# Two more load slots at the start of the experts, and expert steps merged two by two, in a two-layer hybrid decoder

## The chip, the cores and the metric

The kernel runs on one core of a Trainium2 chip. The metric is the time on the device in microseconds. The time before is the median of three runs. The profile is of one execution. PE is TensorE, DVE is VectorE, ACT is ScalarE, POOL is GpSimd, and SP (SyncE) issues nearly all loads.

## The reference

Two layers on 256 tokens of width 1024, in fp32. Each layer has a token mixer (two attention branches behind one input projection, sigmoid gates, one output projection) and a channel mixer: a dense SwiGLU in layer 0, and 8 experts with 2 for each token in layer 1. Behind each sub-layer stands a LayerNorm over the residual.

```
def moe_swiglu(x, w_router, w_gate_up, w_down):
    logits = (x @ w_router).astype(jnp.float32)
    top_v, top_i = lax.top_k(logits, TOP_K)
    gates = jax.nn.softmax(top_v, axis=-1)
    combine = jnp.sum(jax.nn.one_hot(top_i, N_EXPERTS, dtype=jnp.float32) * gates[..., None], axis=-2)
    y = jnp.zeros_like(x)
    for e in range(N_EXPERTS):
        y = y + combine[..., e:e + 1].astype(x.dtype) * swiglu(x, w_gate_up[e], w_down[e])
    return y

for l in range(DEPTH):
    mix = token_mixer(h, w_in[l], ...)
    h = layer_norm(DEEPNORM_ALPHA * h + mix, ln_mix_g[l], ln_mix_b[l])
    f = swiglu(h, ...) if l % 2 == 0 else moe_swiglu(h, ...)
    h = layer_norm(DEEPNORM_ALPHA * h + f, ln_ffn_g[l], ln_ffn_b[l])
```

An expert's gate and up weights are 1024 x 7168, its down weights 3584 x 1024; all eight experts are read, about 350 MB.

## The kernel before

**Products.** Weights arrive as fp32 tiles (`raw`). In the dense layers and for the large experts each tile is split into a high part (`whi`, made on ACT, L433) and the remainder (`wlo`, made on DVE from `raw` and `whi`, L434). An fp32 product is then three fast ones: high by high and high by low of the activations (`xh`, `xl`), and low weights by `xh`. Products with few tokens use `raw` directly with fp32 activations (`xs`), where an instruction shows as two records. Nearly all products have L304, the helper that issues them, so they are told apart by tile names.

**The experts.** The experts of a run are sorted by the number of their tokens into eight places with 192, 128, 128, 64, 64, 32, 32 and 32 token slots (`SLOTS`). The last place always holds expert 7 (`FIXED`), whose weights can be loaded before the routing is known. Places 0, 1 and 2 form the big chain, with split weights; places 7, 6, 5, 4, 3 the small chain, with `raw`. A step of a chain is one load of up to 1 MiB and what is computed with it. Place 0 has 64 of its 192 slots apart (`far`): they are multiplied with `raw` directly, `mm<-raw,xs` with 64 columns, so a big tile's slot is free once its splits and its far product are done.

**Loads.** SP issues the loads in program order; each waits, on SP, until its slot is free. There are nine tiles in a pool of their own (`AHEAD`) and a ring of eight slots of 1 MiB (`RING`). The fixed expert's gate and up weights come as 32 tiles (8 for each of four column groups, `WIDE`): the first half is 16 tiles of 1 MiB, then come tiles of 768 KB. 17 tiles are fetched ahead (L382): seven of the first half and the first of the second in the ring, nine in the other pool. All later loads are from L389. When the first half is done, `self.front` is closed: the space of the nine tiles goes to the pool `parts`, which holds the high parts, while the low parts lie beside the ring in `wp`.

**Order.** The small chain's first eight steps (two tiles each) run first. Then `merge` takes steps of both chains, in proportion, by the counts of `MERGE`: (42 big, 47 small), (50, 14), (42, 46). A scheduler orders the instructions on each engine by priorities and dependences; `in_turn` chains only the products of one step, or of steps that `together` has joined, so steps can pass each other on PE.

**The final LayerNorm's rows.** `spread_rows` (from step 160) loads the weight and bias rows to one partition and multiplies them with a row of ones to get them on 128 partitions (L304, `tp<-ln_gb,one_row`), all four in one go, and ACT copies them out (L1613).

**Fillers.** `keep_busy` issues products whose results nobody reads (`o<-onesb`), in places where PE would stand idle. `out_norm` is the output projection with the LayerNorm behind it: for each of two token tiles statistics, a scale by small steps on DVE (`ln_scale`), then `ln_apply` (L545, L546), transposes and splits into `hT` for the next projection.

Of the kernel before, what the change touches and what calls it, by code (L numbers as in the profile page):

```python
# [9 lines left out]
F32R = mybir.dt.float32r  # L10
# [9 lines left out]
KT = D // 128  # L20
# [13 lines left out]
FIXED = 7  # L34
SLOTS = [192, 128, 128, 64, 64, 32, 32, 32]
UPS = (0, 6, 2, 8, 4, 10, 12)
RING, AHEAD = 8, 9
BRANCH, LEAD = 2, 6
MERGE = ((42, 47), (50, 14), (42, 46))
WIDE = ((0, 4), (7, 4), (4, 3), (11, 3))  # L40
# [39 lines left out]
class Packed:  # L80
# [138 lines left out]
    def last(self, keys, ws, st):  # L219


        nc, b, half = self.nc, self.b, self.half
        back = b.got[self.name][1].bitcast(F32)
        y = self.last_y(self.dn)
        bks = [[b.mm_bank() for _ in range(2)] for _ in range(2)]
        for t in range(2):
            b.in_turn([(bks[h][t], back[half[h], t * 128:(t + 1) * 128], y[half[h]], True, False) for h in range(2)])

        def products(x, ks, w, first, last):
            out = []  # L230
            for i, (r, _, j) in enumerate(ks):
                out += self.times([(x[half[i % 2]], 512 * i, 512)], self.hid[r, j], w, first and i < 2, last and i >= len(ks) - 2)
            b.in_turn(out, [w.load])

        def give(h, t, y):
            cs = slice(h * 512, h * 512 + 512)
            b.mm(bks[h][t], back[:, t * 128:(t + 1) * 128], y, False, True)
            nc.vector.scalar_tensor_tensor(self.acc[t][:, cs], bks[h][t], self.gates[t][:, self.place:self.place + 1], self.acc[t][:, cs],  # L238
                                           op0=OP.mult, op1=OP.add)
            b.ln_stats(self.acc[t], st[t], h)  # L240
        with b.tc.manual_schedule(engines={mybir.EngineType.PE}):
            xs = [b.aux_bank() for _ in range(2)]
            products(xs[0], keys, ws[0], True, True)
            y0 = self.last_y(xs[0])
            products(xs[1], keys[:2], ws[1], True, False)
            give(0, 0, y0)
            products(xs[1], keys[2:], ws[2], False, True)
            y1 = self.last_y(xs[1])
            give(0, 1, y0)
            for t in range(2):  # L250
                give(1, t, y1)
# [18 lines left out]
class Body:  # L270
# [114 lines left out]
    def slot(self, src, split=False):  # L385

        m, n = src.shape[1:]
        raw = self.raw()
        self.loaded = self.nc.sync.dma_start(raw[:, :m * n].rearrange("p (a b) -> p a b", b=n), src)  # L389
        w = Slot(raw, m * n, self.loaded)  # L390
        if split:
            for a in range(0, w.size, 1024):
                n = min(1024, w.size - a)
                both = [pool.tile([128, 1024], F32R, name="w" + p, tag="w" + p, bufs=4) for p, pool in (("hi", self.pp), ("lo", self.wp))]
                for p, x in zip("hl", both):
                    w.part[p].append(x)
                self.parted = self.split(both[0][:, :n], both[1][:, :n], raw[:, a:a + n])
        return w
# [335 lines left out]
    def mixer(self, l, xT):  # L734
# [7 lines left out]
        for i, k0 in enumerate((0, 2, 4, 6)):  # L742
            wpc = self.piece(w[:, k0:k0 + 2, C_FV:C_FV + 520], self.hold if i else self.first)
            for t in range(2):
                for hf in range(2):
                    if i == 0:
                        vps[t, hf] = self.aux_bank() if hf else self.mm_bank()
                    self.tok(vps[t, hf][:, :260], xT, k0, wpc, t, hf * 260, hf * 260 + 260, i == 0, i == 3)
        if l == 0:
            with tc.issue_after(self.made.ins):  # L750
                self.setup_bias()
# [202 lines left out]
    def out_norm(self, h, xT, w, nk, g, b, routed=False):  # L954
# [24 lines left out]
                    self.nc.vector.scalar_tensor_tensor(r[t][:, cs], h[t][:, cs], ALPHA, ps[t, hf], op0=OP.mult, op1=OP.add)  # L979
                    self.ln_stats(r[t], st[t], hf)  # L980

        def norm(t):
            if t == 0:
                out.extend(self.stream("hT"))
            return self.ln_apply(r[t], self.ln_scale(st[t]), gb,
                                 lambda hf: self.put_T([out[0][p, hf] for p in "hl"], r[t][:, hf * 512:(hf + 1) * 512], t))
        order = [(i, hf) for hf in range(2) for i in range(len(cuts))]
        for p in order[:-4]:
# [27 lines left out]
        with self.tc.manual_schedule(engines={mybir.EngineType.PE}):  # L1016
            for i in range(3):
                load(*p[i])
                go(*p[i], 0, 0)
                go(*p[i], 0, 1)  # L1020
            load(*p[3])
            for n, (i, part, t) in enumerate(((0, 0, 1), (0, 1, 1), (1, 0, 1), (3, 0, 0), (3, 1, 0), (1, 1, 1), (2, 0, 1), (2, 1, 1), (3, 0, 1), (3, 1, 1))):
                go(*p[i], t, part)
                for f, *x in behind.get(n, ()):
                    if routed and n == 9:
                        self.keep_busy(3, spare)
                    f(*x)
            self.keep_busy(11 if routed else 3, spare)
        if routed:
            scales = []  # L1030
            lg = self.rt.tile([128, 2, 8], F32, name="lg")
# [11 lines left out]
                self.ln_apply(r[1], scales[1], gb, lambda hf: None)  # L1043
            return r, (hot, routing)
        with self.tc.high_priority():
            self.hold = norm(0)
        self.first, self.late = None, self.hold
        norm(1)
        return r, out[1]


# [216 lines left out]

    def tile_mm(self, outs, x, w, flats, first, last):

        for n, out in enumerate(outs):
            for i, act in enumerate(x):
                for j, part in ((0, "h"), (1, "h")):
                    self.mm(out, act[j], w.at(part, flats[i] + n * 512, 512), first and i + j == 0, False)
        for n, out in enumerate(outs):
            for i, act in enumerate(x):
                self.mm(out, act[0], w.at("l", flats[i] + n * 512, 512), False, last and i == len(x) - 1)

    def together(self, products=(), loads=()):

        products, loads = list(products), list(loads)
        for p, l in self.beside:
            products += p
            loads += l
        self.beside = []
        if products:
            self.in_turn(products, loads)

    def settle(self):

# [4 lines left out]
    def in_turn(self, products, after=()):  # L1295

        made = []
        for x in products:
            self.mm(*x)
            made.append(self.made.ins)  # L1300
        for x in after:
            self.behind(made[0], x.ins, mybir.DependencyClass.Sync)
        for x, y in zip(made, made[1:]):
            self.behind(y, x, mybir.DependencyClass.NoSync)

    def behind(self, ins, other, kind):
        self.tc.add_manual_dep(ins, other.name, mybir.DependencyInfo(kind, mybir.DependencyReason.DATA), reason="order")
# [166 lines left out]
    def moe(self, ctx, h, routing, g, b):  # L1474
# [15 lines left out]

        self.banks(ctx, "experts_ps", mm=4, tp=2, aux=2)
        pool = self.pk = self.wk
        self.ahead(self.wp, "raw", RING, self.tiles[:2 * KT - AHEAD] + self.tiles[2 * KT:RING + AHEAD])
        eidi = next(routing)
        self.put_off, self.nrows = [], 5
        acc = []
        gates = []
        eid = {}
# [29 lines left out]
        def merge(x, y, parts, lead):  # L1528

            i = j = 0  # L1530
            ends = [(sum(p[0] for p in parts[:n + 1]), sum(p[1] for p in parts[:n + 1])) for n in range(len(parts))]
            at = (0, 0)
            for n, (ex, ey) in enumerate(ends):
                ly = ey - (lead if n == len(ends) - 1 else 0)
                while i < ex or j < ey:
                    if i < ex and (i - at[0]) * (ly - at[1]) <= (j - at[1]) * (ex - at[0]):
                        i += 1
                        yield next(x)
                    else:
                        j += 1  # L1540
                        yield next(y)
                at = ex, ey
        big = chain((0, 1, 2), (self.mm_bank, self.tp_bank))
        small = chain((7, 6, 5, 4, 3), (self.aux_bank, self.tp_bank))
# [2 lines left out]
        def both_chains():  # L1547
# [3 lines left out]
                yield next(small)  # L1551
            self.front.close()
            self.pp = self.side(self.later, "parts")
            yield from merge(big, small, MERGE, 8)
        for n, z in enumerate(both_chains()):
            if n == 6:
# [14 lines left out]
            if n == 72:  # L1571
                order.close()
            if n == 160:
                gb = self.spread_rows(g, b)
            if n == 14:
                with tc.issue_after(self.parted[0].ins):
                    for t in range(2):
# [21 lines left out]
    def spread_rows(self, g, b):  # L1599

        nc = self.nc
        one = self.wk.tile([1, 128], F32, name="one_row", bufs=1)
        nc.gpsimd.memset(one, 1.0)
        gb = [[self.pp.tile([128, 512], F32, name="ln_gb", tag="far", bufs=4) for _ in range(2)] for _ in range(2)]
        for row, xs in zip((g, b), gb):
            for hf, x in enumerate(xs):
                nc.sync.dma_start(x[0:1], row[None, hf * 512:(hf + 1) * 512])

        def f():
            for x in gb[0] + gb[1]:  # L1610
                bk = self.tp_bank()
                self.mm(bk, one, x[0:1], True, True)
                nc.scalar.activation(x, bk, AF.Copy)  # L1613
        self.later_on(f)
        return gb

    def overflow(self, h, gates, overi, most, weights, eid, acc):

# [85 lines left out]
    def dense(self):  # L1704
# [28 lines left out]
        h = xs  # L1733
        self.late = last
        for l in range(DEPTH):
            mT, wo = self.mixer(l, hT)
            if l == DEPTH - 1:
                self.tiles = [(p, k) for p in range(len(WIDE)) for k in range(KT)]
                self.ready = {}
                self.ahead(self.side(self.front, "ahead"), "ahead", AHEAD, self.tiles[2 * KT - AHEAD:2 * KT])  # L1740
            h, hT = self.out_norm(h, mT, wo, KT, a["ln_mix_g"][l], a["ln_mix_b"][l], l == DEPTH - 1)
            if l == 0:
                fT = self.ffn(hT)
# [28 lines left out]
```

## Time and profile before

| | |
|---|---|
| median of three runs | 1463.91 us (1463.39 to 1464.29) |
| profiled execution | 1463.79 us, its span 1462.1 us |
| mean granted PE clock | 0.989 |
| PE / DVE / ACT busy | 1399.9 / 812.4 / 655.4 us |
| bytes moved | 453.42 MB, mean 310 GB/s |
| fixed expert's first product | 617.52 us |
| last expert load lands | 1441.1 us |

A busy PE includes modelled ends of pipelined products, so the share alone doesn't say whether PE or the loads set the pace. The page cuts the span into 40 slices, which show the granted clock and the bytes; windows of a few microseconds show the same for a chosen stretch. A row of the timeline joins like instructions: start, time from the first start to the last end, engine, line, tiles, count.

### The profile page before, as it was taken

The numbers are of one execution on the slowest core, as the hardware profiler recorded it, in microseconds if no ns is written. First come the engines' busy times: TensorE is split into PE (matmuls) and PEld (weight loads), VectorE is DVE, ScalarE is ACT, GpSimd is POOL, SyncE is SP. The second block draws the span as 40 slices with busy tenths as digits, with TensorE's granted clock in tenths as the row PEclk, the third lists the DMA queues.
The fourth block names the chain that finished last, engine by engine and source line by source line (L and its number), as shares of the span: only waits on it lengthen the run. The fifth ranks groups of instructions, "written<-read, shape, count | busy, mean of one in ns | idle before, by whom it ended". The sixth has DMA issues, their size and how long they took to land. (4 is left out here: it accounts for less than half of the span.)

```text
span 1462.1 us, 20101 instructions
## 1 busy us (share of the span) xinstructions
PE 1399.9 (96%) x7581; PEld 929.2 (64%) x7581; DVE 812.4 (56%) x1233; ACT 655.4 (45%) x954; POOL 16.9 (1%) x44
## 2 busy tenths in 40 slices
PE   8999999999999999999999999999999999999985
PEld 6878978888788789755444453467675455445531
DVE  7757786665577676624253443377667245344423
ACT  4656546664266663133433332356555233323310
POOL 4000000000000000000000000000000000000000
PEclk9999999999999999999999999999999899999998
DMA  9633546555384347699999999999999899999994
GB/s 297 220 120 135 181 146 205 198 167 207 106 265 151 115 145 300 253 385 407 405 418 415 415 419 422 420 419 418 418 420 420 331 421 409 421 420 420 419 366 189
DMA packets 135767, 453.42 MB, mean 310 GB/s; under 512 B 8079, under 2 KB 63399, under 8 KB 108013
## 3 DMA queue, kind: packets, MB, share of 16 engines
q1 hardware_dynamic: 134872, 450.99, 79.5%
q0 software_dynamic: 784, 1.05, 0.4%
q8 instruction: 62, 1.02, 0.3%
q14 instruction: 45, 0.36, 0.1%
q10 hardware_dynamic: 4, 0.01, 0.0%
HBM read 450.96 MB, written 1.05 MB: 309 GB/s over the span
## 5 line engine op out<-in xcount | busy, mean ns | idle before, releaser
L434 DVE TENSOR_TENSOR wlo<-raw,whi 128x1024 fp32r<-128x1024 f32 (+2 forms) x456 | 516.6, 1161 | 414.7 <-ACT whi L433 402.5
L433 ACT ACTIVATE whi<-raw 128x1024 fp32r<-128x1024 f32 (+2 forms) x456 | 442.1, 1005 | 380.9 <-DMA raw<-in_w_expert_gate_up 140.4
L304 PE MATMUL mm<-hT,whi 128*128 128x512 f32 x672 | 234.8, 398 | 0.0
L304 PE MATMUL aux<-raw,xs 128*32 128x512 f32 (+3 forms) x1280 | 188.1, 552 | 4.3 <-DMA raw<-in_w_expert_gate_up 3.5
L304 PE MATMUL mm<-hT,wlo 128*128 128x256 f32 x672 | 175.8, 281 | 0.0
L304 PE MATMUL mm<-whi,xh 128*128 128x512 f32 x336 | 140.7, 419 | 4.7 <-ACT whi L433 3.4
L304 PEld LDWEIGHTS mm<-hT,whi 128*128 128x128 f32 x672 | 121.5, 188 | 23.8 <-issue 0.7
L304 PE MATMUL mm<-whi,xl 128*128 128x512 f32 x336 | 133.2, 396 | 0.0
L304 PEld LDWEIGHTS mm<-hT,wlo 128*128 128x128 f32 x672 | 126.8, 189 | 9.1 <-issue 2.0
L304 PEld LDWEIGHTS aux<-raw,xs 128*32 128x32 f32 (+1 forms) x1280 | 57.4, 121 | 108.6 <-issue 99.4
L304 PE MATMUL aux<-raw,eh 128*32 128x512 f32 (+1 forms) x560 | 93.0, 604 | 11.3 <-DMA raw<-in_w_expert_down 7.7
L304 PE MATMUL mm<-wlo,xh 128*128 128x512 f32 x336 | 98.7, 402 | 0.8 <-DVE wlo L434 0.7
L304 PEld LDWEIGHTS mm<-whi,xh 128*128 128x128 f32 x336 | 63.4, 189 | 56.6 <-issue 23.2
L304 PE MATMUL mm<-whi,eh 128*128 128x512 f32 x336 | 89.1, 405 | 5.6 <-ACT whi L433 5.6
L304 PEld LDWEIGHTS mm<-whi,eh 128*128 128x128 f32 x336 | 59.7, 188 | 36.7 <-ACT whi L433 18.6
L304 PEld LDWEIGHTS mm<-wlo,xh 128*128 128x128 f32 x336 | 62.2, 189 | 23.1 <-DVE wlo L434 4.6
L304 PEld LDWEIGHTS mm<-whi,xl 128*128 128x128 f32 x336 | 63.5, 189 | 11.7
L304 PEld LDWEIGHTS aux<-raw,eh 128*32 128x32 f32 (+1 forms) x560 | 26.2, 121 | 60.7 <-issue 58.2
L429 ACT ACTIVATE sums<-mm 128x512 f32<-128x512 f32 x84 | 50.2, 600 | 31.9 <-PE mm L304 30.5
L304 PE MATMUL aux<-hT,whi 128*128 128x512 f32 x160 | 56.2, 396 | 0.0
L304 PE MATMUL mm<-raw,xs 128*64 128x512 f32 x224 | 54.2, 605 | 0.0
L304 PE MATMUL mm<-whi,hT 128*128 128x260 f32 (+2 forms) x192 | 50.9, 335 | 1.2 <-DVE hT L434 0.9
(345 smaller groups left out, 1607.8 us busy)
## 6 DMA issues: line engine op xcount, KB each, us to landing
raw<-in_w_expert_gate_up SPq DMA_DIRECT2D x140, 1024.0 KB, 11.9
raw<-in_w_expert_down SPq DMA_DIRECT2D x111, 1024.0 KB, 12.7
raw<-in_w_expert_gate_up SPq DMA_DIRECT2D x112, 768.0 KB, 11.5
raw<-in_w_in SPq DMA_DIRECT2D x36, 1024.0 KB, 5.1
raw<-in_w_ffn_gate_up SPq DMA_DIRECT2D x22, 1024.0 KB, 5.1
raw<-in_w_ffn_down SPq DMA_DIRECT2D x10, 1024.0 KB, 4.9
raw<-in_w_out SPq DMA_DIRECT2D x8, 1024.0 KB, 5.0
raw<-in_w_in SPq DMA_DIRECT2D x8, 520.0 KB, 6.7
```

Of the source, the lines that this page charges most:

```text
L304: self.made = self.nc.tensor.matmul(out, lhsT, rhs, start=start, stop=stop)
L429: self.nc.scalar.activation(x, bank, AF.Copy, scale=scale)
L433: return (self.nc.scalar.activation(hi, src, AF.Copy), self.nc.vector.tensor_sub(lo, src, hi.bitcast(F32)))
L434: self.nc.vector.tensor_sub(lo, src, hi.bitcast(F32)))
```

## The change

Five things change together.

- `EXTRA = 2`: a second pool of two slots holds the last two tiles of the first half, until the first half is done. The nine tiles ahead are those before them, and the ring starts with five tiles of the first half and three of the second. From then on that space is the pool `low`, which holds the low split parts.
- `merge` takes two steps of a chain at a time. `in_line` chains all weight products on PE in program order, where before only the products of a step were chained.
- `spread_rows` splits each row into high and low parts and multiplies these with ones; the four spreads are given out one by one, every fourth step from step 160 on, each one flush behind its split.
- In layer 0's first column group eight fillers stand ahead of the transposes of a token tile. `out_norm` without routing has nine fillers, not three.
- `out_norm` computes the second token tile's scale ahead of the first tile's `ln_apply`.

```
-RING, AHEAD = 8, 9
+RING, AHEAD, EXTRA = 8, 9, 2
...
-                both = [pool.tile([128, 1024], F32R, name="w" + p, tag="w" + p, bufs=4) for p, pool in (("hi", self.pp), ("lo", self.wp))]
+                both = [pool.tile([128, 1024], F32R, name="w" + p, tag="w" + p, bufs=4) for p, pool in (("hi", self.pp), ("lo", self.lo))]
...
+                if l == 0 and i == 2 and t == 0:
+                    self.keep_busy(8, self.o_bank(), self.made)
...
-            self.keep_busy(11 if routed else 3, spare)
+            self.keep_busy(11 if routed else 9, spare)
...
-            self.hold = norm(0)
+            self.hold = norm(0, self.ln_scale(st[0]))
+            scale = self.ln_scale(st[1])
         self.first, self.late = None, self.hold
-        norm(1)
+        norm(1, scale)
...
+    def in_line(self, products, after=()):
+        made = self.in_turn(products, after)
+        if self.line:
+            self.behind(made[0], self.line, mybir.DependencyClass.NoSync)
+        self.line = made[-1]
...
-        self.ahead(self.wp, "raw", RING, self.tiles[:2 * KT - AHEAD] + self.tiles[2 * KT:RING + AHEAD])
+        early = 2 * KT - AHEAD - EXTRA
+        self.ahead(self.wp, "raw", RING, self.tiles[:early] + self.tiles[2 * KT:2 * KT + RING - early])
+        extra = self.front.enter_context(tc.tile_pool(name="extra", bufs=1, reuse_waits="tile"))
+        self.ahead(extra, "extra", EXTRA, self.tiles[2 * KT - EXTRA:2 * KT])
...
-                        i += 1
-                        yield next(x)
+                        for _ in range(min(2, ex - i)):
+                            i += 1
+                            yield next(x)
                     else:
-                        j += 1
-                        yield next(y)
+                        for _ in range(min(2, ey - j)):
+                            j += 1
+                            yield next(y)
...
             self.front.close()
             self.pp = self.side(self.later, "parts")
+            self.lo = ctx.enter_context(tc.tile_pool(name="low", bufs=1, reuse_waits="tile"))
...
-                gb = self.spread_rows(g, b)
+                gb, spreads = self.spread_rows(g, b)
+            if n > 160 and n % 4 == 0 and spreads:
+                self.later_on(spreads.pop(0))
...
-        def f():
-            for x in gb[0] + gb[1]:
-                bk = self.tp_bank()
-                self.mm(bk, one, x[0:1], True, True)
-                nc.scalar.activation(x, bk, AF.Copy)
-        self.later_on(f)
-        return gb
+                def f(x=x):
+                    parts = [self.row_tile("parts", F32R)[0:1] for _ in range(2)]
+                    self.split(*parts, x[0:1])
+
+                    def spread():
+                        bk = self.tp_bank()
+                        self.in_turn([(bk, oner, p, i == 0, i == 1) for i, p in enumerate(parts)])
+                        nc.scalar.activation(x, bk, AF.Copy)
+                    self.later_on(spread)
+                spreads.append(f)
+        return gb, spreads
```

On SP, the loads ahead and the first ones behind them, before. 128x2048 is a tile of the first half, 128x1536 one of the second, 128x2x1024 a tile of the big chain; an ISA row sets up the address of the routed expert.

```order
L382 DMA raw<-in_w_expert_gate_up 128x2048 x16
L382 DMA raw<-in_w_expert_gate_up 128x1536
L1512 TENSOR_LOAD eidi
L1512 ISA x2
L1560 TENSOR_LOAD omaxi
L1560 ISA x2
L389 ISA
L389 DMA raw<-in_w_expert_gate_up 128x2x1024
L389 DMA raw<-in_w_expert_gate_up 128x1536 x3
L389 ISA
L389 DMA raw<-in_w_expert_gate_up 128x2x1024
L389 DMA raw<-in_w_expert_gate_up 128x1536 x2
```

The same place after the change.

```order
L382 DMA raw<-in_w_expert_gate_up 128x2048 x14
L382 DMA raw<-in_w_expert_gate_up 128x1536 x3
L382 DMA raw<-in_w_expert_gate_up 128x2048 x2
L1528 TENSOR_LOAD eidi
L1528 ISA x2
L1579 TENSOR_LOAD omaxi
L1579 ISA x2
L389 ISA
L389 DMA raw<-in_w_expert_gate_up 128x2x1024
L389 ISA
L389 DMA raw<-in_w_expert_gate_up 128x2x1024
L389 DMA raw<-in_w_expert_gate_up 128x1536 x5
```

Two tiles of the second half have moved ahead of the routing, and the second big tile stands directly behind the first. The last two of the five 128x1536 loads take the slots of the two big tiles.

On PE, behind the first half, before. The `aux` products of 32x512 belong to the first half, those of 32x384 to the second; `mm_6275` is the big chain's bank.

```order
L304 MATMUL aux_6187<-raw_5708,xs_6075 32x512 x4
L304 MATMUL aux_6299<-raw_6073,xs_6075 32x384 x4
L304 MATMUL aux_6299<-raw_6297,xs_6075 32x384 x4
L304 MATMUL aux_6299<-raw_6312,xs_6075 32x384 x4
L304 MATMUL aux_6299<-raw_6314,xs_6075 32x384 x4
L148 MATMUL tp_6290<-ident_123,rows_6250 128x128 x4
L304 MATMUL mm_6275<-whi_6267,xh_6139 128x512
L304 MATMUL mm_6275<-whi_6267,xl_6140 128x512
L304 MATMUL mm_6276<-whi_6267,xh_6139 128x512
L304 MATMUL mm_6276<-whi_6267,xl_6140 128x512
L304 MATMUL mm_6289<-raw_6265,xs_6141 64x512 x4
```

After the change, from the end of the second big step on (the first half's last product is followed by 24 products of the two big steps, `mm_6307` and `mm_6308`).

```order
L304 MATMUL mm_6307<-wlo_6332,xh_6167 128x512
L304 MATMUL mm_6307<-wlo_6336,xh_6167 128x512
L304 MATMUL mm_6308<-wlo_6332,xh_6167 128x512
L304 MATMUL mm_6308<-wlo_6336,xh_6167 128x512
L304 MATMUL mm_6321<-raw_6297,xs_6169 64x512 x4
L304 MATMUL mm_6321<-raw_6329,xs_6169 64x512 x4
L304 MATMUL aux_6359<-raw_6090,xs_6103 32x384 x4
L304 MATMUL aux_6359<-raw_6092,xs_6103 32x384 x4
L304 MATMUL aux_6359<-raw_6094,xs_6103 32x384 x4
L304 MATMUL aux_6359<-raw_6368,xs_6103 32x384 x4
```

The second half's tiles have moved from ahead of the first big step to behind the far products of the first two.

On PE, the spread of the rows, before.

```order
L304 MATMUL tp<-ln_gb,one_row 128x512
L304 MATMUL mm<-wlo,xh 128x512 x2
L304 MATMUL tp<-ln_gb,one_row 128x512
L304 MATMUL mm<-wlo,xh 128x512 x2
L304 MATMUL aux<-raw,xs 64x512 x8
```

The same after the change, the first three of four.

```order
L304 MATMUL tp<-parts,one_row_r 128x512 x4
L304 MATMUL mm<-wlo,xh 128x512 x4
L304 MATMUL aux<-raw,xs 64x512 x8
L304 MATMUL tp<-parts,one_row_r 128x512 x2
L304 MATMUL aux<-raw,xs 64x512 x8
```

Each of the four spreads now has two products of split rows; four of the eight stand side by side, and the last spread stands some 70 rows further on.

More of the change, by code (lines that the diff above doesn't have):

```diff
@@ L232, in products @@
                 out += self.times([(x[half[i % 2]], 512 * i, 512)], self.hid[r, j], w, first and i < 2, last and i >= len(ks) - 2)
-            b.in_turn(out, [w.load])
+            b.in_line(out, [w.load])
         def give(h, t, y):
@@ L980, in go, with norm @@
                     self.ln_stats(r[t], st[t], hf)
-        def norm(t):
+        def norm(t, scale):
             if t == 0:
                 out.extend(self.stream("hT"))
-            return self.ln_apply(r[t], self.ln_scale(st[t]), gb,
+            return self.ln_apply(r[t], scale, gb,
                                  lambda hf: self.put_T([out[0][p, hf] for p in "hl"], r[t][:, hf * 512:(hf + 1) * 512], t))
@@ L1269, in tile_mm @@
     def tile_mm(self, outs, x, w, flats, first, last):
+        products = []
         for n, out in enumerate(outs):
             for i, act in enumerate(x):
-                for j, part in ((0, "h"), (1, "h")):
-                    self.mm(out, act[j], w.at(part, flats[i] + n * 512, 512), first and i + j == 0, False)
+                for part in act:
+                    products.append((out, part, w.at("h", flats[i] + n * 512, 512), first and i == 0 and part is act[0], False))
         for n, out in enumerate(outs):
             for i, act in enumerate(x):
-                self.mm(out, act[0], w.at("l", flats[i] + n * 512, 512), False, last and i == len(x) - 1)
+                products.append((out, act[0], w.at("l", flats[i] + n * 512, 512), False, last and i == len(x) - 1))
+        self.in_line(products)
     def together(self, products=(), loads=()):
@@ L1286, in together @@
         if products:
-            self.in_turn(products, loads)
+            self.in_line(products, loads)
     def settle(self):
@@ L1304, in in_turn @@
             self.behind(y, x, mybir.DependencyClass.NoSync)
+        return made
+    def in_line(self, products, after=()):
[3 more added lines that the diff above has]
+        self.line = made[-1]
     def behind(self, ins, other, kind):
@@ L1492, in moe @@
         pool = self.pk = self.wk
-        self.ahead(self.wp, "raw", RING, self.tiles[:2 * KT - AHEAD] + self.tiles[2 * KT:RING + AHEAD])
+        early = 2 * KT - AHEAD - EXTRA
+        self.ahead(self.wp, "raw", RING, self.tiles[:early] + self.tiles[2 * KT:2 * KT + RING - early])
+        extra = self.front.enter_context(tc.tile_pool(name="extra", bufs=1, reuse_waits="tile"))
+        self.ahead(extra, "extra", EXTRA, self.tiles[2 * KT - EXTRA:2 * KT])
         eidi = next(routing)
-        self.put_off, self.nrows = [], 5
+        self.put_off, self.nrows, self.line = [], 5, None
         acc = []
@@ L1603, in spread_rows @@
         nc.gpsimd.memset(one, 1.0)
+        oner = self.wk.tile([1, 128], F32R, name="one_row_r", bufs=1)
+        nc.vector.tensor_copy(oner, one)
         gb = [[self.pp.tile([128, 512], F32, name="ln_gb", tag="far", bufs=4) for _ in range(2)] for _ in range(2)]
+        spreads = []
         for row, xs in zip((g, b), gb):
@@ L1739, in dense @@
                 self.ready = {}
-                self.ahead(self.side(self.front, "ahead"), "ahead", AHEAD, self.tiles[2 * KT - AHEAD:2 * KT])
+                self.ahead(self.side(self.front, "ahead"), "ahead", AHEAD, self.tiles[2 * KT - AHEAD - EXTRA:2 * KT - EXTRA])
             h, hT = self.out_norm(h, mT, wo, KT, a["ln_mix_g"][l], a["ln_mix_b"][l], l == DEPTH - 1)
```

## The prediction

> **What bounds the kernel now.** I read the page first: the sums and the slices. Busy times are in us; section 2 has 40 slices of 36.6 us.
>
> ```profile
> span 1462.1 us, 20101 instructions
> PE 1399.9 (96%) x7581; PEld 929.2 (64%) x7581; DVE 812.4 (56%) x1233; ACT 655.4 (45%) x954; POOL 16.9 (1%) x44
> PEclk9999999999999999999999999999999899999998
> GB/s 297 220 120 135 181 146 205 198 167 207 106 265 151 115 145 300 253 385 407 405 418 415 415 419 422 420 419 418 418 420 420 331 421 409 421 420 420 419 366 189
> ```
>
> PE looks like the bound with 96%, but the bytes tell of two halves. Up to slice 15 (about 560 us) DMA moves 106 to 300 GB/s and PE sets the pace; from slice 18 on nearly each slice has 405 to 422, and one falls to 331. So I read the second half by windows. The columns are the window, its length, busy time of PE, PEld, DVE, ACT and POOL, then the granted clock, DMA's share and GB/s.
>
> ```profile
> 604.00:610.00 6.00, 5.41 (x32) 2.77 (x33) 5.10 (x35) 0.49 (x2) 0.00 (x0) 1.00 1.00 416
> 610.00:618.00 8.00, 8.00 (x65) 7.15 (x67) 6.46 (x26) 2.05 (x8) 0.00 (x0) 1.00 0.02 6
> 620.00:622.00 2.00, 2.00 (x17) 1.04 (x10) 0.00 (x0) 0.00 (x0) 0.00 (x0) 1.00 0.89 334
> 622.00:634.00 12.00, 12.00 (x107) 5.77 (x109) 0.85 (x2) 4.31 (x8) 0.00 (x0) 1.00 1.02 414
> 634.00:636.00 2.00, 2.00 (x28) 1.06 (x24) 1.23 (x2) 1.30 (x2) 0.00 (x0) 1.00 0.42 175
> 636.00:638.00 2.00, 2.00 (x22) 1.14 (x15) 2.00 (x3) 1.70 (x3) 0.00 (x0) 1.00 0.81 227
> 640.00:660.00 20.00, 20.00 (x116) 10.47 (x114) 4.73 (x5) 8.46 (x11) 0.00 (x0) 1.00 1.01 401
> 720.00:740.00 20.00, 20.00 (x110) 8.41 (x110) 10.41 (x11) 8.06 (x10) 0.00 (x0) 1.00 1.01 416
> 1140.00:1160.00 20.00, 20.00 (x62) 8.48 (x62) 7.00 (x6) 6.98 (x8) 0.00 (x0) 0.75 0.71 276
> 1160.00:1180.00 20.00, 19.22 (x83) 9.03 (x82) 6.56 (x6) 8.95 (x12) 0.00 (x0) 1.00 1.00 405
> ```
>
> A DMA share of 1.01 is a full queue: from 640 us to the last load the experts' weights bound the kernel at about 420 GB/s, 2.5 us for a tile of 1 MiB (1.05 MB / 420 GB/s). So an edit counts there by the time in which DMA has nothing to move. There are two such places. At the experts' start DMA rests from 610 to 620.3, and from 634.8 to 636.9 (175 and 227 GB/s of 420 are 0.8 and 1.1 us of transfer). At 1140 to 1160 it loses (420 - 276) / 420 x 20 = 6.9 us, and 0.7 us more in the next 20.
>
> **The start of the experts.** The two extra slots let two more tiles be fetched ahead: 19 loads, not 17, before the routing is known. They wait for no engine and fill part of the rest from 610 on. But slots of the ring that now hold second-half tiles hold no first-half tile, so only five, not seven, come free while PE works on the first half. Loads issued by the end of that half: 17 + 7 = 24 before, 19 + 5 = 24 after, in both cases 22.5 MiB. The early two gain nothing; what counts is when the 25th load starts.
>
> ```profile
> 628.68 7.05 SPq L389 DMA_DIRECT2D raw<-in_w_expert_gate_up  x2
> 633.57 3.67 PE L304 MATMUL aux<-raw,xs 128*32 128x512 f32 x40
> 638.78 1.94 PE L304 MATMUL mm<-raw,xs 128*64 128x512 f32 x8
> 641.69 1.09 PE L304 MATMUL mm<-wlo,xh 128*128 128x512 f32 x4
> 642.61 0.39 PE L304 MATMUL mm<-whi,xh 128*128 128x512 f32 x1
> 634.70 2.95 ACT L433 ACTIVATE whi<-raw 128x1024 fp32r<-128x1024 f32 x3 [3.61 <-PE aux L304]
> 634.77 0.69 DVE L135 TENSOR_TENSOR rows<-aux,gsilu 128x512 f32<-128x512 f32 x1 [9.93 <-PE aux L304]
> 635.38 4.62 DVE L434 TENSOR_TENSOR wlo<-raw,whi 128x1024 fp32r<-128x1024 f32 x4
> ```
>
> The first row is two issues of SP: the 24th load at 628.68, the 25th, held until PE had read the first second-half tile, ending at 635.73, so begun near 635.3. The second row is one 8-record tile of the first half (done near 634.4) and four second-half tiles behind it. The 25th load's bytes begin at 636.9, 1.6 us behind its issue.
>
> After the change PE has two big steps behind the first half, and the second-half tiles behind both. SP's 25th load waits for the slot of the first big step, given back by its far product (the `mm<-raw,xs` x8), which stands behind both steps; SP issues in order, so all later loads wait too. Both big tiles are on chip by then, so the splits set the pace: the last of the four `wlo` ends at 640.0 (635.38 + 4.62), four products with it take 0.9 (641.69 to 642.61), the far product 1.94, the issue 0.3: 643.2, and its bytes flow at 644.8. Against 636.9 that is 7.9 us later, with nothing to make it good while DMA stays the bound; I take +7.8. Ends: +6 if the splits are 2 us earlier (`whi` is done before `wlo` throughout), +11 if both far products (1.94 more) and a second wait behind them count. The low split parts now take the extras' space, and wait for the last first-half tile; the `rows` on DVE ahead of them waits for it already, so that costs nothing here.
>
> **Two by two and in line later on.** A cycle of the first part becomes two big and four small steps, 5 MiB: 12.5 us of DMA. On PE it is 2 x 12 products of 0.23 (5.6), two far products (3.8), and four small of about 0.7 (2.8): 12.2. PE still keeps up, and a slot is held some 4 us longer. That is covered by the queue:
>
> ```profile
> raw<-in_w_expert_gate_up SPq DMA_DIRECT2D x140, 1024.0 KB, 11.9
> ```
>
> 11.9 us from issue to landing is 4.7 tiles of 2.5 us waiting in line. I cost it at nothing; if that cover were under 4 us, each cycle would lose what is missing. Behind the last load the operations stay the same, in the order they have, so the end costs nothing either.
>
> **The spread of the LayerNorm rows.** Next I looked at what stands where DMA loses 7.6 us.
>
> ```profile
> 1132.69 1.12 PE L304 MATMUL tp<-ln_gb,one_row 1*128 1x512 f32 x2
> 1138.44 2.07 PE L304 MATMUL tp<-ln_gb,one_row 1*128 1x512 f32 x2
> 1132.92:1136.33 3.41, 3.41 (x10) 1.40 (x10) 1.74 (x2) 0.91 (x2) 0.00 (x0) 1.00 1.01 413
> 1136.33:1149.98 13.65, 13.65 (x28) 4.70 (x28) 4.63 (x4) 5.27 (x7) 0.00 (x0) 0.50 0.58 229
> 1134.69 0.33 SPq L389 DMA_DIRECT2D raw<-in_w_expert_gate_up  x1
> 1148.47 0.33 SPq L389 DMA_DIRECT2D raw<-in_w_expert_gate_up  x1
> ```
>
> Four fp32 products of one row (two records each; 1.12 us at full clock, 2.07 at half) come close together, 6.4 us in all. Behind them the granted clock is 0.50 for 13.65 us, and SP issues no load for 13.8 us, longer than the 11.9 us of its lead. After the change each spread is two f32r products: eight in all, 1.9 us if each takes the 0.23 of the 512-column products (no row shows a one-row f32r product; the ends are 0.23 and the half of 1.12), and two of the four stand further on. The eight small splits on ACT and DVE (512 elements wide, taken as 0.69 us, like the `rows` above) lie on engines with 45% and 56%; the products of a big step wait for one at most, which the lead covers. PE then loses 1.9 us, not 6.4 plus half of what stood in 13.65; the lead covers that and the hole goes: -7.2 (all of the first window, half of the second); ends -8.2 and -4.
>
> The Trainium skill (TensorE: Matmul & The Clock Gate, "Part 1: The HAM clock gate") says that the clock falls to half after an idle window of about 3.4 us. The lengths agree (3.41 and 13.65 us), but the window ahead of the drop has PE busy 3.41 of 3.41. If that rule were all, the rows would not be its cause, and the half clock would stay.
>
> **Dense layers.** PE sets the pace there, so its idle time counts.
>
> ```profile
> 20.17:23.58 3.41, 1.42 (x11) 1.24 (x12) 3.04 (x5) 0.72 (x2) 0.00 (x0) 1.00 1.10 348
> 23.58:27.00 3.42, 3.42 (x18) 3.42 (x17) 2.52 (x9) 1.82 (x4) 1.79 (x4) 0.50 1.09 356
> 21.29 0.63 PE L477 MATMUL tp<-ident,h 128*128 128x128 f32 x4 [2.18 <-issue]
> 207.30:210.70 3.40, 1.69 (x9) 0.72 (x8) 2.72 (x9) 0.00 (x0) 0.00 (x0) 1.00 0.85 282
> 210.70:214.10 3.40, 2.44 (x15) 1.76 (x16) 3.40 (x10) 2.70 (x4) 0.00 (x0) 1.00 0.30 93
> 208.11 0.82 PE L304 MATMUL o<-onesb 128*128 128x512 bf16 x3
> 210.64 1.32 PE L469 MATMUL tp<-ident,h 128*128 128x128 f32 x8 [1.71 <-DVE h L546]
> 401.76 0.82 PE L304 MATMUL o<-onesb 128*128 128x512 bf16 x3
> 402.42 1.04 PE L469 MATMUL tp<-ident,h 128*128 128x128 f32 x8
> 407.50 0.39 PE L304 MATMUL mm<-wlo,hT 128*128 128x260 f32 x1 [1.61 <-DVE wlo L434]
> ```
>
> In layer 0 eight filler products (0.22 each, 1.8 us) go into the hole of 2.18 ahead of 21.29. The window had PE busy 1.42 of 3.41 us and half the clock followed, which cost 1.7 us of work; behind a window with 1.69 of 3.40 (at 207.3) it stayed at 1.00. So the filler should save it: I take -1.4, ends -1.7 and 0. In `out_norm` nine fillers replace three. At 208.11 they end near 210.1, ahead of 210.64: nothing. At 401.76 the transposes followed at once, and six more push them by 1.3 us; the wait of 1.61 for `wlo` at 407.50 absorbs some of it, but the second scale's small steps now stand on DVE ahead of `hT`. I take +1.0 there, ends -0.8 and +1.9. Together -0.4.
>
> **The sum.** 1463.8 (the profiled execution; span 1462.1, 1.7 around it; the median of the runs is 1463.91) + 7.8 - 7.2 - 0.4 = 1464.0. With the ends of the terms apart, the largest two moving independently: about 1460 to 1468.
>
> **Rivals.**
>
> Faster: the late start is smaller and both clock drops go. If the low end of each term holds, 1463.8 + 6 - 8.2 - 2.5 = 1459.1; if PE, with two big steps of its own at the start, also smooths the windows at 401 (640 to 660) up to 416, 0.7 us in 20 and three such stretches, 1457 to 1459. For it: the hole at 1140 is plain in every column. Against: the +6 needs the splits earlier than their row.
>
> Slower, the lumps: in the second part (50 big, 14 small) the merge now gives six to eight big steps on end, 2.8 us of PE each against 2.5 of DMA, so PE falls back by some 2 us, with two freed slots returning late. From the point at which this exceeds the lead, DMA stops; seven such cycles at 1 us each give 1471. For it: 20.00 of 20 in most windows. Against: the 4.7 tiles in line.
>
> Slower, the clock stays: the half clock at 1136 has another cause and remains. The rows then save only about 4 of the 7.6: 1463.8 + 7.8 - 4 - 0.4 = 1467.2. For it: a half clock also appears where no such row is:
>
> ```profile
> 1300.17:1303.58 3.41, 3.41 (x10) 0.96 (x12) 2.92 (x4) 0.97 (x2) 0.00 (x0) 0.50 1.01 418
> ```
>
> Against: DMA lost nothing there; the drop alone, for one window, is hidden. The Trainium skill's rule on the idle window (TensorE: Matmul & The Clock Gate, Part 1), taken by itself, stands on this side.
>
> No effect: the load order at the start could be so early that the 25th load is not late, and the rest as said: 1463.8 - 7.2 - 0.4 = 1456.2. The in-order queue speaks against it; it joins the faster rival.
>
> **The numbers.** A measurement here tells 0.2% (2.9 us) from no change: faster is under 1461.0, slower over 1466.8. The forecast has 0.40, nearly all within; faster rival 0.30, of which the no-effect case has 0.05; lumps 0.14; clock 0.16. Of the forecast 0.04 fall on the fast side. So faster 0.34, same 0.36, slower 0.30. The range runs from 1457 to 1470, since both signs hold much of the chance; the forecast's own is 1460 to 1468.
>
> **What would show it.** The start: no transfer from about 631 to 644, and the first issue behind the far product near 643, against 635.3. The spread: 1140 to 1160 at 415 GB/s or more and clock 1.00; if the clock is 0.50 with DMA full, it was the lump alone. Layer 0: clock 1.00 at 24 to 27, and what follows 1.4 us earlier. Lumps: a DMA share under 1.00 in windows between 850 and 1030. I am wrong if DMA flows by 638, or if new holes stand behind 660.

## The result, and the profile after

| kernel | median us | runs | ratio to the kernel before, 95% interval |
|---|---|---|---|
| before (runs of the same comparison) | 1462.19 | 6 | 1 |
| changed | 1472.68 (1470.84 to 1475.57) | 6 | 1.0082 (1.0065 to 1.0099) |

The change makes the kernel 0.8% slower, outside the forecast range of 1457 to 1470. The profiled execution took 1475.57 us, 11.8 more than that of before. First the lines of the changed kernel's page that were shown of before.

```profile
span 1473.9 us, 20145 instructions
PE 1393.4 (95%) x7601; PEld 942.0 (64%) x7601; DVE 813.0 (55%) x1238; ACT 656.7 (45%) x958; POOL 16.8 (1%) x44
PEclk9999999999999999999998999999999999999998
GB/s 295 221 141 115 174 177 194 186 173 187 117 266 135 139 144 347 285 251 406 389 417 401 368 381 420 421 418 418 411 420 420 416 420 418 420 420 420 419 360 181
raw<-in_w_expert_gate_up SPq DMA_DIRECT2D x140, 1024.0 KB, 12.7
```

PE does no more work than before (1393.4 us against 1399.9). The slices show it in bytes: the 331 of before is gone (416 now stands there), but slices 17 and 22 to 23 have 251, 368 and 381, where before had 385, 415 and 419. Windows of the changed kernel (columns as before: clock, DMA's share and GB/s last):

```profile
630.00:636.00 6.00, 6.00 (x47) 2.77 (x40) 2.07 (x3) 2.96 (x3) 0.00 (x0) 1.00 0.00 0
636.00:642.00 6.00, 5.68 (x28) 3.58 (x28) 3.16 (x3) 0.60 (x1) 0.00 (x0) 1.00 0.00 0
642.00:646.00 4.00, 4.00 (x36) 1.33 (x36) 0.00 (x0) 0.00 (x0) 0.00 (x0) 1.00 0.58 190
700.00:720.00 20.00, 20.00 (x110) 12.02 (x109) 6.99 (x6) 8.35 (x18) 0.00 (x0) 1.00 0.95 366
800.00:820.00 20.00, 18.71 (x93) 11.44 (x94) 9.36 (x8) 7.87 (x9) 0.00 (x0) 0.91 0.90 350
820.00:840.00 20.00, 19.23 (x108) 9.39 (x106) 9.66 (x12) 7.85 (x10) 0.00 (x0) 1.00 0.97 382
860.00:880.00 20.00, 19.81 (x115) 11.92 (x114) 9.19 (x10) 7.63 (x10) 0.00 (x0) 1.00 0.88 343
1140.00:1160.00 20.00, 19.62 (x82) 14.89 (x84) 17.51 (x20) 10.19 (x12) 0.00 (x0) 1.00 1.01 419
1160.00:1180.00 20.00, 20.00 (x90) 8.86 (x86) 6.99 (x6) 8.82 (x12) 0.00 (x0) 1.00 1.01 413
```

The hole at 1140 has closed. At the start no transfer began for 13.3 us (630.2 to 643.5), and four windows between 700 and 880 have lost bytes that no window of before lost there. A lag in bytes gives the account: for each time of the kernel before, how much later the changed kernel has moved as many bytes, from the ends of all transfers of the two profiled executions.

```
time in before, us    610    640    700    740    800    840    860    880   1140   1180   1400   1440
lag of the change    -1.0   +7.6   +6.7   +8.6   +8.8  +13.8  +17.4  +17.4  +18.2  +10.9  +10.3  +11.8
```

So: dense layers -1.0; start of the experts +7.7 (from -1.0 to +6.7); first part of the merge +10.7 (to +17.4); the rows -7.3; the rest +1.7, 1.5 of it at the end. The sum is 11.8. The first, second and fourth terms are near the forecast's; the one of 10.7 us had been set at nothing. So had the end, and its 1.5 us stay open: e7 below, with the rows alone, has 2.0 there. The prediction's own sign of being wrong, new holes behind 660, came true.

Where it comes from stands in the waits of SP between 640 and 880 us (engine and line, what it waited for, total us, times, longest). Before, then after:

```profile
SPq L389 <- PE aux L304: 139.6, 55, 7.8
SPq L389 <- PE mm L304: 41.6, 32, 3.0
```

```profile
SPq L389 <- PE mm L304: 119.2, 30, 10.0
SPq L389 <- DVE wlo L434: 36.9, 13, 4.2
SPq L389 <- PE aux L304: 29.0, 46, 3.6
```

Before, SP waited mostly for small products (`aux`). Now it waits for the big chain's far products (`mm`), up to 10.0 us at once. Between two issues lie up to 13.3 us now and 8.3 before (read from the issues in the trace): several loads go out in a few microseconds, then none until both steps of a pair and the first far product are done. What such a gap costs depends on the bytes still in line when it begins, that is issued and not yet landed. Both are counted from the issues and transfers of the trace, the bytes taken at 420 GB/s:

```
gap begins at, us            697.6   798.8   827.4   856.8      742.6   760.0   783.4   911.7
without an issue, us          12.2    12.0    11.0    13.3       10.8    10.5    10.5    11.4
in line at its start, us      12.3    10.9    11.2    12.4       15.2    13.0    13.7    16.1
left at its end, MiB          0.13    0.02    0.17    0.00       1.78    0.98    1.25    1.91
```

The four gaps on the left are the four stalls: the line runs empty, or nearly so, before the next load is issued. The four on the right are nearly as long, begin with more bytes in line and cost next to nothing (the lag grows by 0.2 us from 740 to 800).

### The profile page after: what moved, and what is told of

Read it like the earlier page. It is cut to its first block, busy times and chain, and to the rows that moved or that the text cites. A ratio compares the mean times of both kernels' runs of the same rounds, so it can differ in the third digit from the quotient of the medians.

```text
span 1473.9 us, 20145 instructions
## 1 busy us (share of the span) xinstructions
PE 1393.4 (95%) x7601; PEld 942.0 (64%) x7601; DVE 813.0 (55%) x1238; ACT 656.7 (45%) x958; POOL 16.8 (1%) x44
## 5 line engine op out<-in xcount | busy, mean ns | idle before, releaser
L434 DVE TENSOR_TENSOR wlo<-raw,whi 128x1024 fp32r<-128x1024 f32 (+2 forms) x456 | 513.9, 1160 | 384.1 <-ACT whi L433 370.2
L304 PE MATMUL aux<-raw,xs 128*32 128x512 f32 (+3 forms) x1280 | 182.1, 547 | 9.5 <-DMA raw<-in_w_expert_gate_up 9.1
L304 PE MATMUL mm<-wlo,xh 128*128 128x512 f32 x336 | 95.5, 399 | 1.3 <-DVE wlo L434 1.1
L304 PE MATMUL mm<-raw,xs 128*64 128x512 f32 x224 | 51.1, 598 | 0.0
## 6 DMA issues: line engine op xcount, KB each, us to landing
raw<-in_w_expert_gate_up SPq DMA_DIRECT2D x140, 1024.0 KB, 12.7
```

The source lines that it names most:

```text
L304: self.made = self.nc.tensor.matmul(out, lhsT, rhs, start=start, stop=stop)
L434: self.nc.vector.tensor_sub(lo, src, hi.bitcast(F32)))
```

## The experiments

Each ran beside the kernel before, on one chip with the others of its group. The medians of before in the three groups were 1458.81, 1460.55 and 1461.39 us, so the ratios are what compares across groups. My theory is that of the held slots: a pair gives its load slots back late, and SP, which waits in order, issues nothing meanwhile. Its rivals are the chain on PE across steps (the line), the half clock, and lumps of work in every part of the merge.

| run | what it is | median us | ratio, 95% interval |
|---|---|---|---|
| e1 | before + rows + fillers + early second scale | 1457.52 | 0.9986 (0.9975 to 0.9997) |
| e2 | changed, single steps | 1460.36 | 1.0006 (0.9996 to 1.0017) |
| e3 | changed, no chain across steps | 1476.37 | 1.0115 (1.0095 to 1.0134) |
| e4 | changed, far product behind each step | 1469.90 | 1.0070 (1.0050 to 1.0089) |
| e5 | e2 without extra slots | 1460.40 | 1.0006 (0.9991 to 1.0021) |
| e6 | changed without extra slots | 1477.85 | 1.0117 (1.0090 to 1.0145) |
| e7 | before + rows alone | 1458.20 | 0.9983 (0.9972 to 0.9995) |
| e8 | before, a second profile | 1460.57 | one run |
| e9 | changed, far product first | 1462.45 | 1.0007 (0.9996 to 1.0018) |
| e10 | changed, single steps in the first part | 1460.19 | 0.9994 (0.9981 to 1.0008) |
| e11 | e2, far product first | 1459.76 | 0.9990 (0.9978 to 1.0002) |
| e12 | e5, far product first | 1459.54 | 0.9987 (0.9974 to 1.0000) |

**e2, merge by single steps.**

```
-                        for _ in range(min(2, ex - i)):
+                        for _ in range(1):
-                        for _ in range(min(2, ey - j)):
+                        for _ in range(1):
```

> The changed kernel with merge by one step. Theory of the held slots (a pair gives its two slots back only behind both steps' far products, SP waits in order, and the queue runs dry): the stalls of the first part (10.4 us of lag) go, and at the start the first far product comes behind one big step and two small tiles instead of two big steps, some 3 us earlier: 1472.5 - 10.4 - 3 = 1459. Theory of the line (PE can't fill its waits): the stalls stay, 1469 or more. Theory of the clock (idle PE halves the clock, and that starves the slots): steps by one leave shorter idle times, so also near 1460; e4 tells it from the first.

Some 11 us went by the ratios (1.0082 to 1.0006); some 13 were expected. Single steps in line have none of the stalls: the lag stays at 3.9 us from 720 to 1040. The longest time between issues there is 8.4 us (8.3 before). So the chain on PE doesn't make them by itself. This run changes held slots and lumps together and can't tell these two apart.

**e4, each far product directly behind its step.**

```
-        full = len(self.beside) > 1
+        full = len(self.beside) > 0
```

> The changed kernel, steps two by two and in line, but each big step's far product directly behind it instead of both behind the second step. Held slots: the first slot of a pair comes back some 4.7 us earlier (one step of 2.8 and one far product of 1.9), the 25th load starts near 639 instead of 643, and most of the stalls in the first part go: 1460 to 1464. Line or clock as the cause: PE's work, its order in the large and its idle times are nearly as in the changed kernel, so 1469 or more.

It came out on the rivals' side. Of the 10.7 us between 700 and 880 4.5 went (6.2 are left), but the start stayed as late. There the 25th load flowed at 641, and the 26th waited for the second step's far product: DMA rested again from 643.6 to 645.8. Giving back one slot of two doesn't help where SP's next load wants the second. Both big steps still stand ahead of that slot, so e4 couldn't tell the theories apart.

**e9, the far product ahead of the split products.** It needs no splits, so this is a true release: a slot then waits for its splits alone. In the step of a pair (and likewise for the down weights; `step(True)` gives each step out at once, as e4 does):

```
+                side.up_pair(c, k0, w)
+                self.together()
                 self.tile_mm(bks, [x(k0), x(k0 + 1)], w, (0, 1024), k0 == 0, k0 + 2 == KT)
-                side.up_pair(c, k0, w)
-                self.step()
+                self.step(True)
```

> The changed kernel, two by two and in line, but each big step's far product ahead of its split products: it needs no splits, so a slot is free once its splits are made, not behind the step. PE's products and the merge are the same. Held slots: the 25th load starts near 638, the next two each about 1.5 us late, 4 us gained at the start, and most of the 10 us of stalls in the first part go: 1459 to 1465. Lumps of PE's work or the clock as the cause: as e4, where the far product moved less, 1468 or more.

The same products, two by two and in line, but no stalls. Windows of e9, and SP's waits there:

```profile
700.00:720.00 20.00, 20.00 (x105) 9.98 (x102) 6.99 (x6) 6.79 (x10) 0.00 (x0) 1.00 1.02 414
800.00:820.00 20.00, 19.68 (x128) 10.25 (x128) 8.87 (x11) 7.27 (x10) 0.00 (x0) 1.00 1.02 412
860.00:880.00 20.00, 20.00 (x120) 9.09 (x120) 8.15 (x8) 8.29 (x9) 0.00 (x0) 1.00 1.01 413
SPq L389 <- DVE wlo L434: 59.1, 28, 4.7
SPq L389 <- PE mm L304: 42.0, 22, 4.5
```

The far products now hold SP for 42.0 us in all, not 119.2, and for 4.5 at most, not 10.0; the splits hold it for 59.1, not 36.9, but for 4.7 at most. The longest time without an issue from 640 to 880 is 6.0 us, while PE still does two big steps and their far products in one go. The lag grows by 0.1 us from 740 to 860. At the start the 25th load went out at 638.38 and the lag at 640 was 5.2. So the held slots made the stalls.

**e10, single steps in the first part alone.**

```
+                        for _ in range(min(2 if n else 1, ex - i)):
+                        for _ in range(min(2 if n else 1, ey - j)):
```

> The changed kernel, but by single steps in the first part of the merge (the one with far products), and two by two in the second and third. Held slots: big tiles of later places have no far product and there is no start to delay, so this equals e2, 1460 (within 1.5 us). Pairs cost something in every part: 152 of 241 steps are left in pairs, so some 60% of the 12 us between e2 and the changed kernel stay, 1467.

It equals e2 within the intervals. Here two by two costs nothing where no far product holds a slot; the forecast's rival had put the lumps in the second part, where the changed kernel loses 0.8 us (lag 17.4 at 880, 18.2 at 1140).

**e3, no chain across steps** (the two lines of `in_line` that tie a step to the one before it are left out).

> The changed kernel, steps two by two, without the chain on PE across steps. Held slots: the scheduler is free to put the far products, which need no splits, ahead of the low products, so the 25th load starts some 5 us earlier and the stalls shrink, but a pair's slots still come back together: 1460 to 1466. Line: all stalls go, 1457 to 1460. Clock: 1468 or more, the lumps are the same.

The time came out where the theory of the clock had it (1468 or more); those of the slots and of the line missed. The trace divides the loss. The start was earlier (lag 5.3 at 720), but 6.5 us went between 820 and 860. The clock was 1.00 there, and from 852.0 on no load was issued for 11.9 us, against 10.8 us of bytes in line: the scheduler, left free, did not bring the slots back early enough. Then the 5.7 gained at the rows by 1150 were lost again by 1160, where DMA fell to 352 and 215 GB/s:

```profile
1130.00:1140.00 10.00, 6.33 (x25) 3.88 (x24) 10.00 (x14) 5.01 (x7) 0.00 (x0) 0.90 1.01 419
1140.00:1150.00 10.00, 10.00 (x34) 7.89 (x34) 6.93 (x8) 5.18 (x5) 0.00 (x0) 0.76 1.02 414
1150.00:1160.00 10.00, 10.00 (x40) 6.73 (x39) 7.34 (x7) 5.10 (x7) 0.00 (x0) 1.00 0.89 352
1160.00:1170.00 10.00, 10.00 (x42) 3.94 (x41) 2.36 (x2) 2.49 (x3) 0.00 (x0) 1.00 0.63 215
```

PE idles first (6.33 of 10), then runs at less than the full clock, and then DMA runs dry. So with big steps on end the second part can lose time too when the clock falls just there; that the clock is the cause is argued from the order of the rows, no run tests it. Which instructions the scheduler let pass was not followed further.

**e5 and e6, without the extra slots** (`EXTRA` and its two pools taken back).

> e2 without the two extra slots: single steps, in line, rows and fillers as in the changed kernel, 17 loads ahead. If the extra slots only move bytes from the time behind the first half to the time ahead of it, this equals e2, 1460 (within 1 us), since the 25th load waits for the first second-half tile, behind one big step on PE, in both. If the extra slots gain what they hold (2 MiB, 5 us), this is 1465; if they cost, it is at e1's 1457.5.

> The changed kernel without the two extra slots, still two by two and in line. Merge as the cause: late start and stalls of the first part stay, 1471 to 1474, as the changed kernel. Extra slots as the cause of the late start: 6 to 7 us less, 1465.

With single steps the extra slots are worth nothing (1.0006 with and without). With pairs, e6 has the same start (lag +8.7 over its dense layers, against 8.6 in the changed kernel) and 8.2 us of stalls in the first part. So the pairs make the late start and the stalls without the extra slots too. At 1477.85 it lies above the 1471 to 1474 expected: it loses 2.5 us more in the dense layers and a hole of 4.6 us near 1160, both where the clock fell to 0.83 over 10 us; whether the slots have a part in these is open.

**e1 and e7, the rows.**

> The kernel before with only the split spread of the rows, the fillers and the early second scale; no extra slots, no merge by two, no line. All theories agree here: the lag of the changed kernel behind the one before, in bytes, shows -7.2 us at the rows and -1.1 at the dense layers, and those parts stand alone here, so 8 us less than before: ratio 0.9943, some 1454 us.

> The kernel before with the split spread of the rows alone. If the hole at the rows stands in every execution of the kernel before, 7.2 us less: 1451.6. If it is a matter of where the clock's windows fall, and the 1463.79 of the first profile was one of the slow ones, the gain in the median is 1 to 3 us, and the spread of times is smaller: 1456 to 1458, as e1.

> The kernel before, unchanged, for a second profile. If the hole at the rows is in every execution, DMA loses 6.9 us near 1140 again and the time is near 1463. If it depends on the clock, a time near 1457 goes with a shorter half-clock stretch there and a smaller loss.

e1 gained 1.3 us and e7 2.4, not 8 or 7. e8 shows part of the reason; rows of the kernel before, second profile:

```profile
1140.00:1160.00 20.00, 20.00 (x76) 8.64 (x78) 6.99 (x6) 6.91 (x8) 0.00 (x0) 0.91 0.84 327
1140.49 1.12 PE L304 MATMUL tp<-ln_gb,one_row 1*128 1x512 f32 x2
```

The same program at the same place has clock 0.91, where the first profile had 0.75, and moves 327 GB/s, not 276: it loses 4.4 us, not 6.9. The spreads take 1.12 at the end, where they took 2.07. In e7's profile the hole is closed, with lag -7.6 against the first profile; against e8's it is 4.3. Of that, e7's own profile gives up some 2 us in the dense layers, where its code is that of before, and 2 at the end, so the two profiles don't give the median's gain exactly. In the runs of e7's group before ranges from 1456.24 to 1466.23, e7 only from 1457.20 to 1460.53. In the other kernels with split rows and no stalls (e1, e2, e5, e9 to e12) the times lie within 3.2 us of each other too, so the split rows seem to take away the long cases more than they speed up the short ones.

**e11 and e12, versions to keep.**

> e2 (single steps, in line, extra slots) with the far product ahead of the split products. Held slots: the first part has no stalls left to gain, but the 25th load at the start comes some 2 us earlier: 1458. Otherwise 1460, as e2.

> e5 (single steps, in line, no extra slots) with the far product ahead. If the extra slots move bytes only, this equals e11, 1458 (within 1 us); if they matter once slots come back early, it is slower by up to 3 us.

Both are near 1459.6, not the 1458 expected, and equal to each other, as expected of slots that only move bytes. All beat the changed kernel. Against before the gains are small: 0.14% for e1 and 0.17% for e7, and 0.13% for e12, whose interval just reaches 1. e7, the rows alone, is the smallest edit.

## Why the prediction was wrong, step by step

**The start: right.** Forecast +7.8, measured +7.7. The wait was the one named, on the first far product; the rows show the last low parts, their products, the far products and the 25th load:

```profile
634.53 4.62 DVE L434 TENSOR_TENSOR wlo<-raw,whi 128x1024 fp32r<-128x1024 f32 x4
639.60 1.08 PE L304 MATMUL mm<-wlo,xh 128*128 128x512 f32 x4
640.61 3.65 PE L304 MATMUL mm<-raw,xs 128*64 128x512 f32 x16
642.59 0.33 SPq L389 DMA_DIRECT2D raw<-in_w_expert_gate_up  x1
```

The 25th load went out at 642.59, against 643.2 in the forecast, with the first half over 0.8 us sooner; no transfer began from 630.2 to 643.5. One reading was off without changing the sum: the last `wlo` ended at 639.15 and PE came to its products at 639.60, so PE's products set the pace there, not the splits. The extra slots gained nothing, as argued (e5).

**Two by two later on: wrong.** The step that failed is "I cost it at nothing": it measured 10.7 us. The prediction set a hold longer by "some 4 us" against a cover of 11.9 us, the median from issue to landing. But the changed kernel's median is 12.7 and it starves: a median of issues says how long most loads stand in line when they are sent in a burst, and nothing of the time in which none is sent. What decides is how long no load is issued, against the bytes in line when that time begins: 13.3 us against 12.4 in the worst case. The hold was too small as well, since it left out the gathers (`tp<-hot,h`) for the next expert, which stand among the products of a pair at 697.6 and 856.8. The gap from 697.6 on:

```profile
697.49 2.87 PE L304 MATMUL tp<-hot,h 128*128 128x192 f32 x16
702.30 1.46 PE L304 MATMUL tp<-hot,h 128*128 128x192 f32 x8
707.84 3.65 PE L304 MATMUL mm<-raw,xs 128*64 128x512 f32 x16
709.82 2.09 SPq L389 DMA_DIRECT2D raw<-in_w_expert_down  x2
```

Two stretches of gathers (4.3 us), the two big steps and the first far product lie ahead of the load at 709.82. Of the four windows with stalls three have a clock of 1.00, so the clock is not their cause.

**The rows: right in mechanism, mis-sized.** In the two profiles the term is -7.3 against -7.2. The products took 0.30 to 0.37 each, and no half clock followed:

```profile
1157.40 1.19 PE L304 MATMUL tp<-parts,one_row_r 1*128 1x512 f32 x4
1163.21 0.73 PE L304 MATMUL tp<-parts,one_row_r 1*128 1x512 f32 x2
```

But 6.9 was the loss of one execution. In the median of runs the rows alone are worth 2.4 us (1460.55 to 1458.20). The Trainium skill (TensorE: Matmul & The Clock Gate, "What's actually happening") states that the clock's activity window runs free, so that the number of slow products at a kernel's start differs from run to run. The two profiles of before show such a difference in mid-kernel (0.75 and 0.91 in the same 20 us). The Trainium skill's rule (same section) that the clock falls behind an idle window is not all there is to it here: the window ahead was busy with one-row products, and the clock stayed at 1.00 at 1140 to 1180 once they were split.

The fourteen profiles bear the prediction out against the rival in which the clock has another cause. Their half clocks last 3.41 us or a multiple (up to 1440 us). Only three begin behind a window of that length that PE filled wholly, and one-row fp32 products stand in all three: from 1132.9 in the first profile of before, from 1132.0 and 1138.8 in e8. Ahead of every other beginning, that at 1300.17 included, PE had been busy for 2.42 of 3.41 us at most. Splitting the rows doesn't shut out a half clock of that second kind: e3 and e6 have one near 1140, in e6 behind this window, and both lose some 5 us by 1160.

```profile
1140.00:1143.40 3.40, 0.21 (x1) 0.21 (x2) 3.40 (x5) 0.27 (x1) 0.00 (x0) 1.00 1.02 424
```

**The dense layers: right for one pair of profiles, in part by luck.** Forecast -0.4, measured -1.0. In layer 0 the fillers kept the clock, as forecast: none of the eleven profiles with them has a half clock between 15 and 35 us, and the three without them have one each. But nine of the eleven have another near 211 to 225 us, and their lag at 610 is 0.0 to 1.8; only the changed kernel's own and e4's (-0.8) have none there. With the dense layers of before and a half clock there, e8 and e7 have 0.2 and 2.0. In `out_norm` the transposes came 0.4 us later (402.85 against 402.42).

```profile
18.96 1.90 PE L304 MATMUL o<-onesb 128*128 128x512 bf16 x8
24.00:26.00 2.00, 2.00 (x19) 2.00 (x18) 1.54 (x5) 1.74 (x4) 0.41 (x1) 1.00 1.09 348
402.85 1.04 PE L469 MATMUL tp<-ident,h 128*128 128x128 f32 x8
```

**The rivals.** The lumps came near in price (1471, from seven cycles at 1 us), but by luck: the loss is four stalls in the first part, not the second, and comes from slots held by far products. The forecast's sum with them, 1464.0 + 10.7 = 1474.7, is near the profiled 1475.57; the range took their price for an end and not for a term on top.

## What to carry to other kernels

When steps are joined, ask when each load slot is given back and what is queued behind it: the cover is the bytes in line when the issuing engine starts its longest wait, not the median time from issue to landing. If a product that needs no preparation shares a slot with one that does, put it first; here that order took the kernel with pairs from 1.0082 of before to 1.0007. Before a stall of one profile is counted as a gain, look at a second profile of the same kernel, above all if a half clock stands beside it.

## What the runs showed of the hardware

The half clock comes and goes between executions of one program. Near 210 to 220 us the kernel before had the full clock in its first profile and 0.83 in its second. e1, e2 and e6, whose dense layers are those of the changed kernel, had 0.83 in two stretches of 10 us from 210 to 230. Their lag grew by 3.4 to 3.6 us between 220 and 300 us, where the changed kernel's grew by 0.9 at full clock. The difference, some 2.6 us, is more than the 1.5 us that they were ahead at 220.

How little PE must do for the clock to fall doesn't come out of these profiles as one number: a half clock began behind windows of 3.41 us with PE busy for up to 2.42, and none behind some with 1.41 (e1, from 1410.3). The share of time in which PE is busy is not the whole measure, as the one-row products show too.
